# A list schedule with other durations for a hybrid decoder layer on one core

## The chip, the cores and the metric

The kernel runs on one core of one Trainium2 chip. The metric is the time of one execution on the device in microseconds (us). Engines are named as in the profile: PE (TensorE matmuls), PEld (its weight loads), DVE (VectorE), ACT (ScalarE), POOL (GpSimd), SP (SyncE, which here issues the DMAs).

## The reference

One decoder layer over 4096 tokens of width 1024. Three mixers read the same normalised and modulated input and share one input and one output projection:

```python
shift, scale, gate = jnp.split(c_act @ ada_w + ada_b, 3, axis=-1)
h = _rmsnorm(x, g_pre) * (1.0 + scale[:, None]) + shift[:, None]
proj = h @ w_in
aq, ak, av, ag, rkv, rg, gq, gkk, gv, gg = jnp.split(proj, ...)
attn = _sliding_window_attention(aq, ak, av, sinks) * jax.nn.silu(ag)   # window 128, 8 query heads, 2 key heads
rkv = rkv + (_shift(rkv) - rkv) * mu_rkv
rr, rk, rv = jnp.split(rkv, 3, axis=-1)
rwkv = _rwkv7_mixer(h, rr, rk, rv, ...) * jax.nn.silu(rg)               # 4 heads of 64, state 64x64 per head
gla = _gla_mixer(h, gq, gkk, gv, ...) * jax.nn.silu(gg)                 # 4 heads, chunks of 64
y = jnp.concatenate([attn, rwkv, gla], axis=-1) @ w_out
return x + gate[:, None] * _rmsnorm(y, g_post)
```

The RWKV mixer is a recurrence over tokens, `S = S * w + (S @ -kk) (kk*a) + v k`, with output `S @ r`; the kernel computes it in chunks of 64 tokens.

## The kernel before, in words

The 4096 tokens are cut into 16 tiles of 256. The program has two phases. Phase 1 (to about 1215 us) runs the two recurrent mixers for all tiles and, between their operations, turns the remaining weights into pairs of f16 slices for phase 2. Phase 2 computes attention, the gates and the output projection, one tile per period of about 65 us.

Names that are used below, in phase 1:

- `xt` is a tile of x (1 MB by DMA). `hf` are its squares (sums `ssx`) and later its scaled values, `msx`, `nwi`, `rsx`, `nwt` are the twelve small DVE operations of a reciprocal square root, `tp` its transposes on PE, `hT` the transposed normalised input as two f16 parts, stored in `hscr` for phase 2.
- `lp`, `zz`, `pv`, `gqk` are projections of hT on PE (weights as two f16 parts, so three matmuls for each slice). They share one ring of PSUM banks. `zb` is zz after the token shift (DVE); a bank is free for the next projection when zb is done.
- `gp`, `ga`, `gl`, `cgp` are the forget gate of GLA: gp (PE), ga (three ACT operations with a table load among them), gl (DVE), cgp its cumulative sum (PE).
- RWKV for each chunk: `atp` and `AT` (products within the chunk), `sp`, `Ss`, `Sst` (the state), `rp`, `rs`, `up`, and `UV` (ACT copies of up and vp, read by sp and `bp`). `T`, `TT`, `Xp`: the inverse of a triangular block. `tsc` and `TT` are its substitution on DVE, 30 small operations for a tile; it reads `AS`, which is AT's diagonal blocks sent through DRAM (`adr`) and back by DMA, with its diagonal set to one by POOL.
- `yt`, `ot`, `np`: transposes and norms of the outputs. `gap`, `kvp`, `op`, `Gst`: GLA's products and state.
- `cs`, `ch`, `cl`: a slice of weights by DMA, its high and low f16 part. The first ACT operation on cs, its square with a sum, is also named ch. `aw`, `acc`: the adaLN matrix (1 MB blocks, summed on POOL).
- `wps`, `gw`, `cw`: decay of RWKV.

In phase 2: `qp`, `kp`, `q`, `kT` (queries and keys), `sc`, `pr` (scores), `gp`, `gh`, `ag`, `mx`, `mT` (gates and mixed values), `op`, `yv` (output projection), `oi` (scale).

Every instruction goes through one helper (line 299 in the profile), so groups are told apart by tile names. The program is written by generators ("streams"), one for a stage of a tile; which generator goes on is set by a small model, and this order of writing is not what the engines run. `Order.note` records each instruction with a planned duration (`occ` is how long its engine is held, `lat` when its result is there), the instructions that it needs, and its tile's turn in a buffer. `Order.pin` then runs a list schedule over these records: it takes the engine that can begin first, picks the earliest recorded instruction that is ready, and ties each instruction to the one before it on its engine. So every engine's row is fixed by the table of durations; the instructions and their number are not. `pin` is called once for phase 1 and once for phase 2. The first stage of phase 2 is not pinned.

In the planner PE has tilings: 64x64 products occupy one quarter of the array, 128x128 products all of it, written (2, 2) and (4, 4) in units of 32. A change costs 0.094 us in the plan.

Of the kernel before, what the change touches and what calls it, by code (L numbers as in the profile page):

```python
# [31 lines left out]
HOP, VL, AL, PL = 0.4, 0.2, 0.2, 0.06  # L32
EXP_TABLE, LN_TABLE = 1, 2
LIFT = {}
LANES = ((0.06, 1.04e-3, VL), (0.02, 1.0e-3, AL), (0.1, 2.3e-3, 0.0), (0.0, 1e-3 / 2.4, PL), (0.05, 0.0, 2.0))

SIZE = {F16: 2, BF16: 2, F32: 4, I32: 4}
ENGINES = ("PE", "DVE", "Activation", "Pool", "SP")
HOP_FROM = {"PE": 0.037, "DVE": 0.034, "Activation": 0.034, "Pool": 0.06, "SP": 0.03}
HOP_INTO = {"PE": 0.02, "Pool": 0.04, "SP": 0.03}  # L40


# [12 lines left out]
class Step:  # L55


    __slots__ = ("ins", "eng", "occ", "lat", "table", "array", "bytes", "needs", "turn", "start", "end", "left", "then")


class Order:
# [1 line left out]


    def __init__(self, tc):
        self.tc, self.held, self.masks = tc, {}, {}
        self.steps = []
        self.wrote, self.read, self.users, self.slots, self.known = {}, {}, {}, {}, set()

# [25 lines left out]
    def note(self, eng, name, outs, ins, func, r):  # L95

        st = Step()
        st.ins, st.eng, st.table, st.array, st.bytes, st.then = r.ins, str(eng.engine).split(".")[-1], None, None, 0, []
        e, o = st.eng, outs[0]
        on_psum = [a for a in ins if str(a.tensor.space) == "PSUM"]  # L100
        n = max(math.prod(a.shape[1:]) for a in [o, *ins[:1]])
        cols = len([a for a in ins[1:] if math.prod(a.shape[1:]) == 1]) if n > 1 else 0
        if e == "PE":
            f32, lhs = ins[0].dtype == F32, self.region(ins[0])
            n = math.prod(o.shape[1:])
            _, p0, p1, _ = self.region(o)
            rows, cs = (lhs[1] // 32, (lhs[2] + 31) // 32), (p0 // 32, (p1 + 31) // 32)
            rows, cs = [(0, 4) if b - a > 2 else (a, b) for a, b in (rows, cs)]
            mode = (rows[1] - rows[0], cs[1] - cs[0])
            took = n * (2 if f32 else 1) / 2400 + 0.003  # L110
            took = max(took, 0.056 if not f32 else 0.109 if mode[1] == 4 else 0.0)
            issue = 0.007 if not f32 or mode == (4, 4) else 0.009 if mode == (1, 1) else 0.16 if mode == (2, 4) else 0.03
            cells = [4 * a + b for a in range(*rows) for b in range(*cs)]
            st.array = (mode, cells, 2 if f32 and name == "matmul" else 1, took, issue)
            st.occ = st.lat = 0.0
        elif e == "SP":
            st.bytes = math.prod(ins[0].shape) * SIZE[ins[0].dtype]
            kb = st.bytes / 1024
            st.occ = 0.47
            st.lat = next((t for k, t in ((8, 1.9), (64, 2.0), (128, 2.2), (256, 2.6), (512, 3.5)) if kb <= k), 4.8)  # L120
        elif e == "Activation":
            st.occ = (0.05 if on_psum else 0.093) + 0.093 * (len(ins) - 1) + 0.832e-3 * n
            st.lat = st.occ + 0.1
            if len(outs) > 1:
                st.occ += 0.187
                st.lat = st.occ + 0.02
            st.table = LN_TABLE if func == AF.Ln else EXP_TABLE if func in (AF.Exp, AF.Tanh) else None
        elif e == "Pool":
            if name == "memset":
                st.occ = 0.06  # L130
            elif name == "tensor_copy":
                st.occ = 0.25 if n <= 2 else 0.11 + 0.95e-3 * n
            else:
                st.occ = 0.42 + 1.35e-3 * n if n <= 256 else 1.95e-3 * n
            st.lat = st.occ + 0.05
        else:
            if name == "tensor_reduce":
                n = math.prod(ins[0].shape[1:])
            fast = name in ("tensor_scalar", "tensor_single_scalar") and not on_psum and o.dtype == F32
            fixed, rate = 0.065 + 0.06 * (cols > 0), 1.04e-3  # L140
            if fast:
                rate = 0.53e-3
            elif name == "transpose":
                fixed = 0.09
            elif name == "memset":
                fixed, rate = 0.05, 0.3e-3
            elif name == "tensor_tensor" and len(o.shape) == 3 and o.shape[2] <= 16 and n > 16:
                fixed, rate = 0.09, 1.55e-3
            st.occ = fixed + rate * n
            st.lat = st.occ + 0.085  # L150

        k, st.needs, st.turn = len(self.steps), {}, []
        out_r, in_r = [self.region(a) for a in outs], [self.region(a) for a in ins]
        tiles = {a.tensor.name: a.tensor for a in [*outs, *ins]}

        def need(j, data=False):
            st.needs[j] = st.needs.get(j, False) or data

        for t, tensor in tiles.items():
            if t not in self.known:  # L160
                self.known.add(t)
                if t in self.held and tensor.tag:
                    held = self.slots.setdefault((tensor.owner_uid, tensor.tag), [])

                    if held and self.users.get(held[-1]):
                        st.turn.append(self.users[held[-1]][0])
                    if len(held) == self.held[t]:
                        for j in self.users.get(held.pop(0), ()):
                            need(j)
                    held.append(t)  # L170
            elif t in self.held and self.users.get(t):
                st.turn.append(self.users[t][0])
            if str(tensor.space) == "PSUM":
                for j in self.users.get(t, ()):
                    need(j)

        def meet(a, b):
            return a[1] < b[2] and b[1] < a[2] and (a[3] is None or a[3] & b[3])

        def covered(a, b):  # L180
            return b[1] <= a[1] and a[2] <= b[2] and (a[3] is None or not a[3] & ~b[3])

        for a in in_r:
            for w, j in self.wrote.get(a[0], ()):
                if meet(a, w):
                    need(j, True)
        for a in out_r:
            if a[3] is not None:
                for old in (self.wrote, self.read):
                    for w, j in old.get(a[0], ()):  # L190
                        if meet(a, w):
                            need(j)
                    old[a[0]] = [(w, j) for w, j in old.get(a[0], ()) if not covered(w, a)]
            self.wrote.setdefault(a[0], []).append((a, k))
        for a in in_r:
            self.read.setdefault(a[0], []).append((a, k))
        for t in tiles:
            self.users.setdefault(t, []).append(k)
        st.needs.pop(k, None)
        self.steps.append(st)  # L200
# [7 lines left out]
    def pin(self):  # L208
# [7 lines left out]
            if not st.left:  # L216
                ready[st.eng][k] = 0.0
        free = dict.fromkeys(ENGINES, 0.0)
        cells, mode, table, pipe = [0.0] * 16, None, None, 0.0
        last = {}  # L220
        for _ in steps:
            e = min((e for e in ENGINES if ready[e]), key=lambda e: max(free[e], min(ready[e].values())))
            now = max(free[e], min(ready[e].values())) + 1e-9
            k = min(k for k, t in ready[e].items() if t <= now)
            st, t = steps[k], max(free[e], ready[e].pop(k))
            if e == "PE":
                m, at, passes, took, issue = st.array
# [5 lines left out]
                    cells[c] = t + passes * took  # L233
                free[e], st.end = t + issue * passes, t + passes * took + 0.165
            else:
                if st.table is not None and st.table != table:
                    t, table = max(t, free[e] + 1.28), st.table
                free[e], st.end = t + st.occ, t + st.lat
                if st.bytes > 100e3:
                    pipe = max(pipe, t + 1.7) + st.bytes / 310e3  # L240
                    st.end = max(st.end, pipe)
            st.start = t
# [21 lines left out]
class Model:  # L264


    def __init__(self, tc):
        self.tc, self.lift, self.order = tc, 0, Order(tc)
        self.wrote, self.read, self.banks = {}, {}, {}
        self.now = 0.0  # L270

# [14 lines left out]
class Lane:  # L286
# [6 lines left out]
    def __getattr__(self, name):  # L293
        f = getattr(self.eng, name)

        def call(*args, **kw):
# [4 lines left out]
            aps = [a for a in (*args, *kw.values()) if isinstance(a, bass.AP)]  # L301
            outs = [aps[0].tensor.name] + ([kw["accum_out"].tensor.name] if kw.get("accum_out") is not None else [])
            accum = kw.get("accum_out")
            self.model.order.note(self.eng, name, aps[:1] + ([] if accum is None else [accum]),
                                  [a for a in aps[1:] if a is not accum], next((a for a in args if isinstance(a, AF)), None), r)
            m, t = self.model, self.clock if self.serial else self.model.now
# [50 lines left out]
def hybrid_kernel(ctx, tc, x, vecs, rows, adaw, w1, wl, w2, wo, w2aug, a2, gk2, cst, ctr, ctg, abias, out):  # L357
# [149 lines left out]
    def emit():  # L507

        while live:
# [10 lines left out]
            assert best is not None, [(s[2], s[1], s[4]) for s in live]  # L520
            PE.clock = max(PE.clock, when)
            model.now = PE.clock
            model.lift = LIFT.get(best[2], 0)
            need = next(best[3], done)
            if need is done:
                done.add((best[2], best[1]))
# [1280 lines left out]
```

## Time and profile before

| | before |
|---|---|
| median of 3 runs | 2227.8 us (2226.26 to 2230.65) |
| profiled execution, its own time | 2226.16 us |
| its span, first to last instruction | 2224.4 us |
| mean granted TensorE clock | 0.983 |
| PE busy | 2063.7 us (93%) |
| DVE busy | 1513.7 us (68%) |
| ACT busy | 1111.6 us (50%) |
| POOL busy | 191.6 us (9%) |
| ACT table loads | 65, 1283 ns each |

A timeline row reads: start in us, duration, engine, line, operation, what it writes and reads, shapes, count, and in brackets how long the engine had been idle before it and what ended that. In a row of waits the numbers are the total in us, how often, and the longest.

### The profile page before, as it was taken

Reading aid. Unit: us, or ns where it says so; the run is one execution under the profiler, and the core shown is the slowest. Engines: PE = TensorE matmul, PEld = TensorE weight load, DVE = VectorE, ACT = ScalarE, POOL = GpSimd, SP = SyncE. Lnnn points to the kernel's source line nnn. Section 1 sums busy time; section 2 is a strip of 40 time slices with the busy share of each in tenths; the row PEclk is TensorE's granted clock in tenths of the full one; section 3 lists DMA queues with packets and bytes.
Section 4 is the critical chain, followed back from the end, with each engine's and each line's share of the span. In section 5 each row is a group of like instructions: output and inputs, shape, how many; then the busy total and the mean of one; then the engine's idle time right before and its main releaser. Section 6 shows DMA issues by size and latency. Waiting matters only on the chain. (4 is left out here: it accounts for less than half of the span.)

```text
span 2224.4 us, 61651 instructions
## 1 busy us (share of the span) xinstructions
PE 2063.7 (93%) x25417; PEld 1755.6 (79%) x25417; DVE 1513.7 (68%) x4970; ACT 1111.6 (50%) x2627; POOL 191.6 (9%) x364
## 2 busy tenths in 40 slices
PE   1599999999999999999997999999999999999996
PEld 1478877777777777787776888888888888888885
DVE  7767787777778777666665676666666666666764
ACT  3566666676766765555423434343434434343441
POOL 0241100111111111111000000000000000000000
PEclk9899999999999999999998999999999999999998
DMA  7332233323233322102324121222221121212111
GB/s 292 118 100 94 80 97 100 97 88 111 77 103 102 97 90 71 54 16 76 124 76 137 63 89 51 70 70 76 71 78 62 56 68 67 78 69 80 61 42 38
DMA packets 149092, 188.46 MB, mean 85 GB/s; under 512 B 49458, under 2 KB 120648, under 8 KB 142408
## 3 DMA queue, kind: packets, MB, share of 16 engines
q1 hardware_dynamic: 146776, 182.23, 24.9%
q8 instruction: 201, 3.29, 0.6%
q10 hardware_dynamic: 2032, 2.26, 0.3%
q14 instruction: 83, 0.68, 0.1%
HBM read 126.75 MB, written 57.68 MB: 83 GB/s over the span
## 5 line engine op out<-in xcount | busy, mean ns | idle before, releaser
L299 PEld LDWEIGHTS <-mT 128*128 128x128 f16 x3072 | 301.3, 98 | 40.1 <-ACT mT L299 2.6
L299 ACT ACTIVATE pr<-pr,nm,lsc 128x256 f32<-128x256 f32 (+1 forms) x256 | 149.3, 585 | 88.7 <-DVE nm L299 86.7
L299 ACT ACTIVATE ag<-gp,gh 128x512 f32<-128x512 f32 x64 | 43.6, 682 | 185.5 <-PE gp L299 185.4
L299 PEld LDWEIGHTS <-hT 128*128 128x128 f16 x1536 | 119.5, 100 | 18.9 <-DVE hT L299 1.0
L299 DVE CUSTOM_DVE_ANT_0 pr<-sc,ab,sinks 128x256 f32<-128x256 f32 (+1 forms) x256 | 107.8, 477 | 37.6 <-PE sc L299 35.9
L299 DVE SCALAR_TENSOR_TENSOR ag<-ag,gp 128x512 f32<-128x512 f32 x64 | 43.5, 679 | 110.7 <-ACT ag L299 110.6
L299 PE MATMUL pv<-gvh,hT 128*128 128x272 f16 x512 | 100.4, 287 | 0.7 <-DVE hT L299 0.4
L299 PE MATMUL lp<-hT,Lh 128*128 128x256 f16 x512 | 96.1, 279 | 2.4 <-ACT vg L299 2.4
L299 PE MATMUL op<-o0h,mT 128*128 128x256 f16 x512 | 93.4, 276 | 3.6 <-ACT mT L299 2.5
L299 PE MATMUL zz<-hT,kh 128*128 128x256 f16 x512 | 92.3, 276 | 0.0
L299 PE MATMUL gp<-hT,q3h 128*128 128x256 f16 x512 | 88.0, 278 | 3.6 <-PEq L1669 3.6
L299 PE MATMUL op<-o3h,mT 128*128 128x256 f16 x512 | 91.4, 273 | 0.0
L299 ACT ACTIVATE jy<-yv 128x1024 f16<-128x1024 f32 x32 | 33.8, 1057 | 114.0 <-DVE yv L299 114.0
L299 PE MATMUL gqk<-hT,gqkh 128*128 128x256 f16 x512 | 88.1, 273 | 1.9 <-DVE zb L299 1.9
L299 PE MATMUL qp<-hT,q1h 128*128 128x256 f16 x512 | 85.5, 274 | 4.2 <-DVE kT L299 4.2
L299 PE MATMUL op<-o2h,mT 128*128 128x256 f16 x512 | 89.3, 273 | 0.0
L299 PE MATMUL op<-o1h,mT 128*128 128x256 f16 x512 | 89.1, 273 | 0.0
L299 POOL COPY kT<-kT 128x512 f16<-128x512 f16 x15 | 10.1, 676 | 909.6 <-DVE kT L299 853.1
L299 PE MATMUL zz<-hT,rh 128*128 128x256 f16 x512 | 86.7, 273 | 0.0
L299 PE MATMUL zz<-hT,vh 128*128 128x256 f16 x512 | 86.4, 273 | 0.0
L299 ACT ACT_TABLE_LOAD x65 | 83.4, 1283 | 5.4 <-DMA sinks<-in_rows 4.2
L299 PE MATMUL gp<-hT,q4h 128*128 128x256 f16 x512 | 85.7, 273 | 0.0
(385 smaller groups left out, 6318.8 us busy)
## 6 DMA issues: line engine op xcount, KB each, us to landing
xt<-in_x SPq DMA_DIRECT2D x16, 1024.0 KB, 5.0
hscr<-hT SPq DMA_DIRECT2D x16, 1024.0 KB, 7.0
hT<-hscr SPq DMA_DIRECT2D x16, 1024.0 KB, 4.8
xo<-in_x SPq DMA_DIRECT2D x16, 1024.0 KB, 5.5
out<-yv SPq DMA_DIRECT2D x32, 512.0 KB, 3.0
cs<-in_w SPq DMA_DIRECT2D x112, 128.0 KB, 2.2
stg<-in_adaw SPq DMA_DIRECT2D x8, 1024.0 KB, 7.6
cs<-in_wo SPq DMA_DIRECT2D x64, 128.0 KB, 2.2
```

Source lines behind the costliest of these rows:

```text
L299: r = f(*args, **kw)
```

## The change

Only the planner's numbers and its rule of choice change; the instructions are the same. A result that lands by DMA is planned 0.6 us later than its landing, instead of 0.03. The landing times of small DMAs are finer. All DMAs, not only those over 100 KB, go through one queue of 310 KB/us in the plan. On ACT and DVE an instruction that works on another half of the partitions than the one before it is planned 0.115 us later. On PE, a ready instruction of the tiling in force is taken before an earlier one of another tiling, unless the array is in tiling (4, 4) and another has waited for 0.6 us. `LAG` is empty, so `rank` is the order of recording.

```diff
+LAG = {}
+TILING_WAIT = 0.6
-HOP_FROM = {"PE": 0.037, "DVE": 0.034, "Activation": 0.034, "Pool": 0.06, "SP": 0.03}
+HOP_FROM = {"PE": 0.037, "DVE": 0.034, "Activation": 0.034, "Pool": 0.06, "SP": 0.6}
...
+        st.half, st.rank = None, len(self.steps) + self.lag
...
-            st.lat = next((t for k, t in ((8, 1.9), (64, 2.0), (128, 2.2), (256, 2.6), (512, 3.5)) if kb <= k), 4.8)
+            st.lat = next((t for k, t in ((8, 1.9), (32, 2.0), (128, 2.3), (256, 2.6), (512, 3.5)) if kb <= k), 4.8)
...
+        if e in ("Activation", "DVE"):
+            st.half = (out_r[0][1], in_r[0][1] if e == "Activation" and in_r and out_r[0][2] - out_r[0][1] <= 64 else None)
...
-            k = min(k for k, t in ready[e].items() if t <= now)
+            at = sorted((k for k, t in ready[e].items() if t <= now), key=lambda k: (steps[k].rank, k))
+            k = at[0]
+            if e == "PE" and mode is not None and steps[k].array[0] != mode:
+                same = [q for q in at if steps[q].array[0] == mode]
+                wait = max(now - ready[e][q] for q in at if steps[q].array[0] != mode)
+                if same and (mode != (4, 4) or wait < TILING_WAIT):
+                    k = same[0]
...
+                if st.half is not None:
+                    was, half[e] = half.get(e, st.half), st.half
+                    if was[0] != st.half[0] or None not in (was[1], st.half[1]) and was[1] != st.half[1]:
+                        t = max(t, free[e] + 0.115)
...
-                if st.bytes > 100e3:
+                if st.bytes:
                     pipe = max(pipe, t + 1.7) + st.bytes / 310e3
```

In phase 1 about 13% of PE's rows, 19% of DVE's, 16% of ACT's and 12% of SP's stand elsewhere than before. In phase 2 the rows of PE, ACT, POOL and SP are the same, and DVE's differ in one row of each period and two more at the second tile. Three places (L299 and L317 are the same helper line in the two files):

ACT around the gate `ga` of a middle tile (the one that ran at 597 us), before:

```order
L299 ACTIVATE ch_8947,wss8_8665<-cs_8881 128x256
L299 ACTIVATE ch_9005,wss8_8665<-cs_8949 128x256
L299 ACTIVATE ch_9077,wss8_8665<-cs_9007 128x256
L299 ACTIVATE ga_8871<-gp_8914 128x256
L299 ACTIVATE ga_8871<-ga_8871 128x256
L299 ACT_TABLE_LOAD
```

and in the change:

```order
L317 ACTIVATE ch_8947,wss8_8665<-cs_8881 128x256
L317 ACTIVATE ga_8871<-gp_8914 128x256
L317 ACTIVATE ch_9005,wss8_8665<-cs_8949 128x256
L317 ACTIVATE ga_8871<-ga_8871 128x256
L317 ACTIVATE hf_8942<-tp_8937,sh_77,gs_76 128x256
L317 ACT_TABLE_LOAD
```

The first ga stands ahead of two squares that wait for DMAs of cs. At the same place on PE, before:

```order
L299 MATMUL up_8974<-rs_8934,tf0_503 64x64 x4
L299 LDWEIGHTS Lh_329
L299 MATMUL lp_8840<-hT_7822,Lh_329 128x256
L299 MATMUL cgp_8981<-CTG_139,gl_8869 128x129 x2
L299 MATMUL tp_8995<-ident_63,xt_8688 128x128 x4
```

and in the change, where twelve lp follow up_8974, of which the last is shown:

```order
L317 LDWEIGHTS Ll_330
L317 MATMUL lp_8840<-hT_7822,Ll_330 128x256
L317 MATMUL vp_9043<-ident_63,zb2_8420 128x128 x4
L317 MATMUL cgp_8981<-CTG_139,gl_8869 128x129 x2
L317 MATMUL tp_8995<-ident_63,xt_8688 128x128 x4
```

Eleven lp and a group of vp moved ahead of cgp.

DVE around the state `Sst` of the tile that ran at 420 us, before:

```order
L299 TENSOR_TENSOR Ss_5821<-sp_5816,Sst1_495 128x128
L299 TENSOR_TENSOR tsc_5737<-TT_5735,AS_5731 128x8x2
L299 TENSOR_TENSOR Sst0_494<-Ss_5821,cd_3960 128x128
L299 TENSOR_REDUCE TT_5735<-tsc_5737 128x8
L299 TENSOR_TENSOR tsc_5737<-TT_5735,AS_5731 128x8x3
```

and in the change:

```order
L317 TENSOR_TENSOR Ss_5821<-sp_5816,Sst1_495 128x128
L317 TENSOR_REDUCE wss_5843<-wss8_5337 128x1
L317 TENSOR_TENSOR Sst0_494<-Ss_5821,cd_3960 128x128
L317 TENSOR_TENSOR qb_5306<-gap_5848,gmask_132 128x256
L317 TENSOR_TENSOR qb_5306<-gap_5849,gmask_132 128x256
L317 TENSOR_TENSOR tsc_5737<-TT_5735,AS_5731 128x8x2
L317 COPY rs_5867<-rp_5854 128x128
```

Sst and two qb stand ahead of the first tsc, and rs right behind it instead of fourteen rows later. The tile at 354 us has the same exchange of Sst and tsc.

DVE in the second tile's start (about 120 to 133 us), before:

```order
L299 TENSOR_TENSOR nwt_1309<-rsx_1307 128x2
L299 SCALAR_TENSOR_TENSOR nwt_1309<-nwt_1309,msx_1305 128x2
L299 SCALAR_TENSOR_TENSOR zb0_912<-zz_913,mu_c_467,zs_993 128x256 x2
L299 TENSOR_TENSOR cd_1046<-ep_967,em_968 128x2x3
L299 COPY cd_1046<-ep_967 128x2
L299 COPY em0_1047<-em_968 128x2
L299 SCALAR_TENSOR_TENSOR rsx_1307<-nwt_1309,rsx_1307 128x2
```

and in the change:

```order
L317 SCALAR_TENSOR_TENSOR nwt_1309<-nwt_1309,msx_1305 128x2
L317 SCALAR_TENSOR_TENSOR rsx_1307<-nwt_1309,rsx_1307 128x2
L317 TENSOR_SCALAR xt_1195<-xt_1195,rsx_1307 128x1024
L317 SCALAR_TENSOR_TENSOR zb0_912<-zz_913,mu_c_467,zs_993 128x256 x2
L317 TENSOR_TENSOR cd_1046<-ep_967,em_968 128x2x3
```

zb0 moved behind the rest of the chain and the first half of xt's scaling. On SP at that time, before:

```order
L299 DMA aw_525<-in_adaw 128x2048
L299 DMA aw_537<-in_adaw 128x2048
L299 DMA xt_1195<-in_x 128x2x1024
L299 DMA gscr_72<-gr_521 1x256
L299 DMA aw_549<-in_adaw 128x2048
L299 DMA hscr_71<-hT_732 128x4096
```

and in the change:

```order
L317 DMA aw_525<-in_adaw 128x2048
L317 DMA xt_1195<-in_x 128x2x1024
L317 DMA aw_537<-in_adaw 128x2048
L317 DMA gscr_72<-gr_521 1x256
L317 DMA hscr_71<-hT_732 128x4096
L317 DMA aw_549<-in_adaw 128x2048
```

Two aw blocks went behind the load of xt and the store of hT.

More of the change, by code (lines that the diff above doesn't have):

```diff
@@ L55 @@
 class Step:
-    __slots__ = ("ins", "eng", "occ", "lat", "table", "array", "bytes", "needs", "turn", "start", "end", "left", "then")
+    __slots__ = ("ins", "eng", "occ", "lat", "table", "array", "bytes", "half", "rank", "needs", "turn", "start", "end", "left", "then")
 class Order:
     def __init__(self, tc):
-        self.tc, self.held, self.masks = tc, {}, {}
+        self.tc, self.held, self.masks, self.lag = tc, {}, {}, 0
         self.steps = []
@@ L218, in pin @@
         free = dict.fromkeys(ENGINES, 0.0)
-        cells, mode, table, pipe = [0.0] * 16, None, None, 0.0
+        cells, mode, table, pipe, half = [0.0] * 16, None, None, 0.0, {}
         last = {}
@@ L267, in __init__ @@
     def __init__(self, tc):
-        self.tc, self.lift, self.order = tc, 0, Order(tc)
+        self.tc, self.lift, self.stage, self.order = tc, 0, None, Order(tc)
         self.wrote, self.read, self.banks = {}, {}, {}
@@ L303, in call @@
             accum = kw.get("accum_out")
+            self.model.order.lag = LAG.get(self.model.stage, 0)
             self.model.order.note(self.eng, name, aps[:1] + ([] if accum is None else [accum]),
@@ L522, in emit @@
             model.now = PE.clock
-            model.lift = LIFT.get(best[2], 0)
+            model.lift, model.stage = LIFT.get(best[2], 0), best[2]
             need = next(best[3], done)
```

## The prediction

> **What bounds the kernel now.** I read the page's busy times and slices first, then windows along the span, then the engines' waits, then short timelines.
>
> ```profile
> PE 2063.7 (93%) x25417; PEld 1755.6 (79%) x25417; DVE 1513.7 (68%) x4970; ACT 1111.6 (50%) x2627; POOL 191.6 (9%) x364
> ```
>
> ```profile
> 60.00:120.00 60.00, 39.86 (x248) 30.37 (x247) 40.87 (x73) 34.88 (x58) 22.52 (x13) 0.83 0.38 140
> 540.00:600.00 60.00, 58.04 (x812) 47.79 (x809) 45.93 (x169) 39.54 (x93) 7.39 (x18) 1.00 0.33 101
> 660.00:720.00 60.00, 56.18 (x731) 46.07 (x723) 46.25 (x171) 41.01 (x92) 7.83 (x16) 1.00 0.32 99
> 1320.00:1380.00 60.00, 59.75 (x705) 53.37 (x704) 38.01 (x109) 25.44 (x65) 0.61 (x1) 1.00 0.18 58
> ```
>
> PE is the bound: 2063.7 us busy, 93% of the span. A window's row reads: stretch, length, then busy time and count of PE, PEld, DVE, ACT and POOL, granted clock, DMA share, GB/s. In phase 2 (1320:1380) PE has 0.25 us of 60 to give. In the middle of phase 1 it has 2 to 4 us of 60, and at 60:120 20 us. Only PE's order, and what PE waits for, can move the time; the instruction lists are the same, so PE's work is the same except for tiling switches and clock. What PE waited for between 120 and 1190 us (total, times, longest):
>
> ```profile
> PE cgp L299 <- DVE gl L299: 7.3, 6, 2.7
> PE rp L299 <- DVE Sst L299: 5.3, 3, 2.8
> PE yt L299 <- DVE ysb L299: 5.1, 4, 3.7
> PE Xp L299 <- DVE T L299: 4.6, 6, 0.9
> PE atp L299 <- DVE RA L299: 4.1, 4, 1.5
> PE ot L299 <- DVE osb L299: 3.3, 5, 1.0
> PE bp L299 <- ACT UV L299: 3.2, 7, 0.5
> PE sp L299 <- ACT UV L299: 2.3, 8, 0.3
> ```
>
> **Part 1: cgp and the recurrence in the middle tiles.** One such tile, at 597 to 601 us, PE, DVE and ACT:
>
> ```profile
> 597.81 0.38 PE L299 MATMUL lp<-hT,Lh 128*128 128x256 f16 x2
> 598.23 1.10 PE L299 MATMUL atp<-RA,KB 64*64 64x128 f32 x32
> 600.87 0.71 PE L299 MATMUL cgp<-CTG,gl 128*128 128x129 f32 x4 [1.10 <-DVE gl L299]
> 601.42 0.60 PE L299 MATMUL tp<-ident,xt 128*128 128x128 f32 x4
> 601.86 0.27 PE L299 MATMUL lp<-hT,Lh 128*128 128x256 f16 x1
> 601.97 0.27 PE L299 MATMUL lp<-hT,Ll 128*128 128x256 f16 x1
> ...
> 600.39 0.42 DVE L299 SCALAR_TENSOR_TENSOR gl<-gp,ga 128x256 f32<-128x256 f32 x1 [2.65 <-ACT ga L299]
> 600.74 1.28 DVE L299 TENSOR_TENSOR AT<-atp,rmask 128x512 f32<-128x512 f32 x2
> ...
> 596.73 0.42 ACT L299 ACTIVATE ch<-cs 128x256 f16<-128x256 f32 x1 [1.57 <-DMA cs<-in_wo]
> 598.65 1.28 ACT L299 ACT_TABLE_LOAD   x1
> ```
>
> The chain is: a weight slice cs lands, ACT squares it (ch, in order), then ga, a table load, ga, then DVE gl, then PE cgp. ACT sat 1.57 us at ch with ga queued behind it. Now ga stands one to two squares earlier, and on PE twelve lp and a group of four vp stand ahead of cgp instead of one lp. Successive lp start 601.97 - 601.86 = 0.11 us apart, so eleven more are 1.2; four transposes took 601.86 - 601.42 = 0.44. So PE has 1.6 us more to do, against waits of 0.3 to 2.7: most vanish. bp and sp (3.2 + 2.3), behind ACT's UV copies, likewise get lp and zz groups ahead of them. These three rows hold 12.8 us; I take **-10.0** (bounds 0, if ga waits elsewhere as long, and -12.8). Xp is placed as before and keeps its 4.6. What is late next is gl itself: the second AT (the pair took 1.28 us) now stands ahead of gl on DVE. Before, DVE sat idle for 2.65 us there, which covers it; without that cover gl is up to 0.65 late.
>
> **Part 2: the state Sst at two tiles.** DVE's tsc reads AS, which comes by DMA behind a whole xt load:
>
> ```profile
> 420.13 0.18 DVE L299 TENSOR_TENSOR tsc<-TT,AS 128x16 f32<-128x16 f32 x1 [4.20 <-POOL AS L299]
> 420.23 0.28 DVE L299 TENSOR_TENSOR Sst<-Ss,cd 128x128 f32<-128x128 f32 x1
> ...
> 419.98 0.12 POOL L299 MEMSET AS<- 128x16 f32 x1 [7.85 <-DMA AS<-adr]
> ...
> 420.57 0.37 PE L299 MATMUL rp<-Sst,RA 64*64 64x64 f32 x1 [2.80 <-DVE Sst L299]
> 424.70 0.69 PE L299 MATMUL up<-rs,tf 64*64 64x64 f32 x8
> ```
>
> Sst needed nothing but its turn, and stood behind tsc. Now it stands ahead, at this tile and at that of 354 us (PE waited 2.23 there), so both waits go. rs then stands behind the first tsc, so up can start shortly after 420.13 + 0.28 + 0.2, some 0.9 us after PE has done what stands before it; I give back 1.4 for both. After each wait the granted clock is at half:
>
> ```profile
> 355.00:356.00 1.00, 1.00 (x6) 0.28 (x3) 0.86 (x5) 0.77 (x2) 0.00 (x0) 0.50 0.21 74
> ...
> 422.00:423.00 1.00, 1.00 (x3) 0.61 (x3) 0.98 (x4) 0.00 (x0) 0.00 (x0) 0.50 0.01 4
> 425.00:426.00 1.00, 1.00 (x12) 0.76 (x9) 1.00 (x5) 0.52 (x2) 0.00 (x0) 0.50 0.00 0
> ```
>
> It is down from about 354.5 to 358 and from 420.5 to 426; half the rate over 3.5 and 5.5 us loses 4.5. So -5.0 - 4.5 + 1.4, taken as **-8.0** (bounds -3, if short waits remain and the clock falls all the same, and -9.5). The Trainium skill (TensorE: Matmul & The Clock Gate, part 1 on the clock gate) says that TensorE falls to half rate after an idle window of about 3.4 us and comes back after a busy one. By that rule waits of 2.2 and 2.8 us need not drop the clock, nothing of the 4.5 would belong to these waits, and the sum would be 4.5 us higher; the rows show half clock right behind them, so the trace decides for counting it, and the 3.5 us of the first stretch agree with the rule's length.
>
> **Part 3: the other waits of phase 1.** yt, atp and ot hold 12.5 us. In the new order one atp and one ot find filler ahead of them, the others stand as before: half, 6, and 2 from the small rows that I don't show. **-8.0** (bounds 0 and -14).
>
> **Part 4: tilings.** PE changes tiling 661 times instead of 671. Three lp up to the change to atp took 598.23 - 597.81 = 0.42 us, where three steps of 0.11 are 0.33, so a change is about 0.09: **-0.9**. The changes of half on DVE and ACT stay within five of what they were, and table loads stay at 65: nothing.
>
> **Part 5: the start.** Up to 97 us the order is the same. Then:
>
> ```profile
> 80.08 3.57 DVE L299 TENSOR_SCALAR msx<-ssx 128x2 f32<-128x2 f32 x1
> 83.68 0.17 DVE L299 TENSOR_SCALAR nwi<-msx 128x2 int32<-128x2 int32 x1
> ...
> 79.21 4.41 POOL L299 TENSOR_TENSOR aw<-aw,scol 128x2048 f32<-128x2048 f32 x1 [65.62 <-DMA aw<-in_adaw]
> ...
> 96.92 0.48 PE L299 MATMUL tp<-ident,xt 128*128 128x128 f32 x1 [13.79 <-DVE xt L299]
> ...
> 120.61 1.03 DVE L299 TENSOR_SCALAR msx<-ssx 128x2 f32<-128x2 f32 x1 [2.54 <-ACT hf L299]
> 128.30 0.87 DVE L299 SCALAR_TENSOR_TENSOR zb<-zz,mu_c,zs 128x256 f32<-128x256 f32 x2
> 131.56 1.42 DVE L299 TENSOR_SCALAR xt<-xt,rsx 128x1024 f32<-128x1024 f32 x2
> ```
>
> Operations on two elements a row take 0.17 us alone and up to 3.57 beside POOL's aw products, and end when a product ends (83.65 and 83.62). In the second burst of products (114 to 130 us) five of the chain's twelve ran before zb, which freed the bank that PE's gqk waited for (1.9 us). Now all twelve and one half of the xt scaling (0.71) stand ahead of zb, and two of the aw loads are issued later, so the burst starts later too. If the burst spares the chain, zb comes at 128.30 + 7 x 0.2 + 0.71, or 2.1 us late; if it stretches the rest of the chain as it did the first, up to 9. PE's other work covers some: **+4.0** (bounds +1 and +13, the latter with the half clock that the first pause left).
>
> **Part 6: phase 2.** PE's, ACT's and POOL's order is the same. On DVE one q subtract stands one small operation earlier in each period, and once a kT subtract stands behind the second yv:
>
> ```profile
> 1283.37 1.23 DVE L299 TENSOR_TENSOR yv<-yv,xo 128x1024 f32<-128x1024 f32 x1
> ...
> 1283.40 0.39 PE L299 MATMUL qp<-hT,q1h 128*128 128x256 f16 x2 [0.30 <-DVE kT L299]
> ```
>
> PE waits for that kT already, so **+1.2**, once (bounds 0 and +2.5).
>
> **Part 7: waits that the new order makes.** Not in this trace. Up to 0.65 a tile by the AT of part 1 in six tiles, of which I take a third, 1.3, and one pair of AT (1.28) elsewhere: **+3.0** rounded up (bounds +1 and +9).
>
> Sum: -10.0 - 8.0 - 8.0 - 0.9 + 4.0 + 1.2 + 3.0 = **-18.7**. The profiled execution took 2226.16 us, so 2207.5; the median of the runs, 2227.8, stands 1.6 above it, so **2209** in the runs' terms. About 0.2%, 4.5 us, can be told from no change here.
>
> **Rivals.**
> (a) The waits move and are not saved. In a list schedule each engine's row is one long compromise: where cgp finds its filler, the lp used for it are missing later. For it: PE had work for every wait that went, so the later stretches are thinner by that work; Xp and most of the tail are unchanged. Against it: over 540:1080 PE has slack only in those short waits. Then parts 1 and 3 fall to a quarter, -4.5 instead of -18, and the time is 2222.5; with the start at its dear end it is no change.
> (b) The start collides in full: +13 instead of +4. For it: the first burst did just that, 13.79 us. Against it: before, half of the second burst was over when the chain began. The time is 2218. [...]
> (c) More goes: every wait of parts 1 to 3 to its bound, start +1, 2226.2 - 12.8 - 9.5 - 14 - 0.9 + 1 + 1.2 + 1, or 2192, 2194 in the runs' terms.
> (d) Slower: ACT's grouping by half and its longer view of landings make the UV copies of the recurrence stand behind a pair of hf or a table load (1.28 us), tile after tile. UV feeds sp, then Ss, Sst, rp, rs, up, and back: a delay of 1.28 plus one hf (about 0.55) is 1.8 a tile, times 16 tiles 29 us, so 2238. It decides from 18.7 / 16 = 1.2 us a tile. Against it: ACT's count of half changes hardly moves, and the UV copies stand among the same neighbours in the rows that I compared.
>
> **How the numbers follow.** The forecast, with parts 1 to 3 mostly as summed, 0.66; (a) 0.13; (b) 0.07; (c) 0.06; (d) 0.08. Faster by over 0.2%: the forecast, (b), (c) and a small part of (a), 0.80. Within 0.2%: most of (a), 0.11. Slower: (d) and a rest for what I don't see, 0.09. The range leaves out (d) and the far ends: 2194, which is (c), to 2226, where (a) ends.
>
> **What would show it.** Right: waits of cgp, bp and sp under 4 us together between 120 and 1190; no wait of rp for Sst near 352 and 418, and clock 1.00 in the windows behind them; phase 2's period unchanged with PE at 59.7 of 60; the gqk wait at 130 us longer than 1.9. Wrong: the same slack per 60 us at 540 to 900 under other names; a new wait of over 5 us at 115 to 140 with half clock after; UV copies late in every tile.

## The result, and the profile after

The changed kernel takes 2203.0 us (median of 4 runs, 2198.2 to 2208.7) against 2227.4 (4 runs): a ratio of 0.9889, 95% interval 0.9863 to 0.9915. The profiled execution took 2203.83 us. In two of the three later sessions, each on a chip of its own, the same pair gave 0.9880 (0.9853 to 0.9906) and 0.9885 (0.9867 to 0.9903). The forecast was 2209, with a range of 2194 to 2226.

The page's busy line after:

```profile
PE 2058.5 (93%) x25417; PEld 1757.3 (80%) x25417; DVE 1504.4 (68%) x4970; ACT 1109.4 (50%) x2627; POOL 198.3 (9%) x364
```

and the windows for the same stretches:

```profile
60.00:120.00 60.00, 41.00 (x273) 31.43 (x274) 43.99 (x78) 37.46 (x65) 20.10 (x12) 0.80 0.37 140
540.00:600.00 60.00, 58.94 (x815) 48.95 (x813) 45.94 (x168) 40.77 (x98) 9.96 (x20) 1.00 0.31 92
660.00:720.00 60.00, 58.93 (x814) 48.74 (x809) 46.58 (x168) 41.40 (x98) 9.82 (x20) 1.00 0.32 99
1320.00:1380.00 60.00, 59.74 (x706) 53.40 (x704) 40.75 (x123) 25.92 (x66) 0.61 (x1) 1.00 0.21 72
```

The counts of instructions are the same. In the middle of phase 1 PE idles 1.1 us of 60, where it was 2.0 and 3.8; phase 2 is as it was. PE's waits between 120 and 1190 us after:

```profile
PE gp L317 <- issue: 5.0, 1, 5.0
PE ovp L317 <- DVE pr L317: 4.9, 3, 2.8
PE Xp L317 <- DVE T L317: 4.4, 5, 0.9
PE up L317 <- DVE rs L317: 3.4, 4, 1.2
PE yt L317 <- DVE ysb L317: 3.1, 3, 1.8
PE atp L317 <- DVE RA L317: 2.7, 4, 1.2
PE ot L317 <- DVE osb L317: 2.6, 4, 1.0
PE kp L317 <- ACT ysb L317: 2.1, 3, 1.0
...
PE rp L317 <- DVE Sst L317: 1.1, 3, 0.7
PE cgp L317 <- DVE gl L317: 1.0, 1, 1.0
```

cgp fell from 7.3 to 1.0, rp<-Sst from 5.3 to 1.1, and bp and sp (5.5 together) are gone from the list. up<-rs and kp<-ysb have grown. The row of ovp is the start of phase 2, which now falls into this window; before, ovp waited 5.2 us for pr, after 1190. A wait of gp for "issue" (time in which the engine waited for nothing that the profile shows), 5.0 us at one place, is new. The kind of wait is not: the list of before has

```profile
PE Xq L299 <- issue: 3.0, 2, 2.6
```

of which the 2.60 us stand at 1096.7, in the tail of phase 1.

Where the time went is read by comparing the start of the same instruction in the two timelines (the last cgp of a tile in phase 1, mp in phase 2):

| | before, us | after, us | difference |
|---|---|---|---|
| first cgp | 107.9 | 105.9 | -2.0 |
| third cgp | 210.7 | 207.5 | -3.2 |
| sixth | 403.9 | 392.7 | -11.2 |
| eleventh | 731.2 | 711.6 | -19.6 |
| last cgp | 1050.1 | 1021.0 | -29.1 |
| first mp of phase 2 | 1235.2 | 1212.6 | -22.6 |
| last mp | 2186.8 | 2164.4 | -22.4 |

Some 2 us a tile are won over all of phase 1, 29 by its last gate. From there to the first mp 6.5 are given back: 5.7 in the tail of phase 1 (to the first ovp, 1192.9 before and 1169.5 after) and 0.8 in the first stage of phase 2. The rest of phase 2 changes nothing.

A middle tile after (ACT, DVE, PE):

```profile
582.10 0.38 ACT L317 ACTIVATE ga<-gp 128x256 f32<-128x256 f32 x1 [2.16 <-PE gp L317]
582.38 0.41 ACT L317 ACTIVATE ch<-cs 128x256 f16<-128x256 f32 x1
583.65 1.28 ACT L317 ACT_TABLE_LOAD   x1
...
584.06 1.29 DVE L317 TENSOR_TENSOR AT<-atp,rmask 128x512 f32<-128x512 f32 x2 [1.56 <-PE atp L317]
585.40 0.42 DVE L317 SCALAR_TENSOR_TENSOR gl<-gp,ga 128x256 f32<-128x256 f32 x1
...
585.48 0.60 PE L317 MATMUL vp<-ident,zb 128*128 128x128 f32 x4
585.91 0.67 PE L317 MATMUL cgp<-CTG,gl 128*128 128x129 f32 x4
```

ga now waits for its own input and no longer for a weight slice; DVE works at AT in the time in which it sat idle; and vp fills PE up to cgp, which waits for nothing.

The state after, at the two tiles with the late AS: the first tsc still waits for it (1.48 and 1.05 us), but Sst has long gone:

```profile
341.65 0.29 DVE L317 TENSOR_TENSOR Sst<-Ss,cd 128x128 f32<-128x128 f32 x1
345.71 0.18 DVE L317 TENSOR_TENSOR tsc<-TT,AS 128x16 f32<-128x16 f32 x1 [1.48 <-POOL AS L317]
345.80 0.28 DVE L317 COPY rs<-rp 128x128 f32<-128x128 f32 x1
409.67 0.18 DVE L317 TENSOR_TENSOR tsc<-TT,AS 128x16 f32<-128x16 f32 x1 [1.05 <-POOL AS L317]
```

and the clock stays whole in the windows behind them:

```profile
350.00:355.00 5.00, 5.00 (x61) 4.33 (x61) 4.79 (x20) 1.79 (x6) 0.10 (x1) 1.00 0.00 0
415.00:420.00 5.00, 5.00 (x65) 4.19 (x64) 4.79 (x27) 2.19 (x6) 0.19 (x1) 1.00 0.01 3
```

The start after (DVE, POOL, PE):

```profile
116.13 0.17 DVE L317 TENSOR_SCALAR msx<-ssx 128x2 f32<-128x2 f32 x1 [1.79 <-ACT hf L317]
116.93 3.45 DVE L317 SCALAR_TENSOR_TENSOR nwt<-nwt,msx 128x2 f32<-128x2 f32 x1
124.50 0.87 DVE L317 SCALAR_TENSOR_TENSOR zb<-zz,mu_c,zs 128x256 f32<-128x256 f32 x2
...
116.75 3.62 POOL L317 TENSOR_TENSOR aw<-aw,scol 128x2048 f32<-128x2048 f32 x1 [3.68 <-DMA aw<-in_adaw]
...
125.42 0.38 PE L317 MATMUL gqk<-hT,gqkh 128*128 128x256 f16 x2 [0.79 <-DVE zb L317]
```

POOL had to wait 3.68 us for its aw block, which is loaded later, and its burst starts at 116.75 instead of 114.15. The first four small operations of the chain run at 0.17 us, two of the twelve are stretched (3.45 and 2.20), and zb comes at 124.5 instead of 128.3. The chain itself starts earlier, at 116.13 instead of 120.61. Part of that is the order of ACT, where the second square of xt stood behind ep before, which waited for PE, and now follows the first square:

```profile
118.88 0.39 ACT L299 ACTIVATE ep<-cw 128x260 f32<-128x260 f32 x1 [1.63 <-PE cw L299]
119.43 1.06 ACT L299 ACTIVATE hf<-xt 128x1024 f16<-128x1024 f32 x1
...
114.95 1.06 ACT L317 ACTIVATE hf<-xt 128x1024 f16<-128x1024 f32 x1
```

And the place in the tail that gives time back, PE and the DMA queues in two windows before it ended:

```profile
1122.27 0.86 PE L317 MATMUL Xq<-td,Xs 32*32 32x32 f32 x64
1128.18 0.58 PE L317 MATMUL gp<-hT,q4h 128*128 128x256 f16 x2 [5.05 <-issue]
```

```profile
q1 hardware_dynamic: 264, 0.96, 89.1%
...
q1 hardware_dynamic: 364, 0.45, 61.3%
q8 instruction: 1, 0.02, 3.0%
```

The first of these rows is 1121 to 1125, the other two are 1125 to 1127. PE waited for no semaphore. From 1119 on, three loads of 512 KB (q5l, q6h, q6l) keep the DMA engines busy (89% from 1121 to 1125, without a packet of instructions); then one packet of the instruction queue passes, in the window that ends 1.2 us before PE goes on. The granted clock is 0.50 from 1128 to 1134, so the place costs 5 us and about 3 more. The 2.60 us of the kernel before look the same: two loads of 512 KB (q3h, q3l) and a store are in flight up to 1094, then one packet of the instruction queue passes (1094.3 to 1095.2), and PE goes on at 1096.74.

### The profile page after: what moved, and what is told of

Its sections match the earlier page's. It is cut to its first block, busy times and chain, and to the rows that moved or that the text cites. A ratio compares the mean times of both kernels' runs of the same rounds, so it can differ in the third digit from the quotient of the medians.

```text
span 2202.1 us, 61608 instructions
## 1 busy us (share of the span) xinstructions
PE 2058.5 (93%) x25417; PEld 1757.3 (80%) x25417; DVE 1504.4 (68%) x4970; ACT 1109.4 (50%) x2627; POOL 198.3 (9%) x364
## 5 line engine op out<-in xcount | busy, mean ns | idle before, releaser
L317 PEld LDWEIGHTS <-mT 128*128 128x128 f16 x3072 | 301.4, 98 | 39.2 <-ACT mT L317 2.6
L317 ACT ACTIVATE pr<-pr,nm,lsc 128x256 f32<-128x256 f32 (+1 forms) x256 | 149.3, 585 | 87.8 <-DVE nm L317 87.1
L317 ACT ACTIVATE ag<-gp,gh 128x512 f32<-128x512 f32 x64 | 43.7, 682 | 188.2 <-PE gp L317 188.2
L317 PEld LDWEIGHTS <-hT 128*128 128x128 f16 x1536 | 118.2, 99 | 19.0 <-DVE hT L317 1.5
L317 DVE CUSTOM_DVE_ANT_0 pr<-sc,ab,sinks 128x256 f32<-128x256 f32 (+1 forms) x256 | 107.8, 477 | 37.3 <-PE sc L317 35.6
L317 DVE SCALAR_TENSOR_TENSOR ag<-ag,gp 128x512 f32<-128x512 f32 x64 | 43.4, 678 | 111.3 <-ACT ag L317 111.3
L317 PE MATMUL pv<-gvh,hT 128*128 128x272 f16 x512 | 98.6, 284 | 1.8 <-DVE kg L317 0.8
L317 PE MATMUL lp<-hT,Lh 128*128 128x256 f16 x512 | 94.9, 279 | 3.0 <-ACT vg L317 3.0
L317 PE MATMUL op<-o0h,mT 128*128 128x256 f16 x512 | 93.5, 276 | 2.8 <-ACT mT L317 2.5
L317 PE MATMUL gp<-hT,q3h 128*128 128x256 f16 x512 | 89.0, 280 | 7.5 <-issue 4.0
L317 PE MATMUL zz<-hT,kh 128*128 128x256 f16 x512 | 93.6, 274 | 0.0
L317 PE MATMUL gp<-hT,q4h 128*128 128x256 f16 x512 | 87.5, 277 | 5.0 <-issue 5.0
L317 POOL COPY kT<-kT 128x512 f16<-128x512 f16 x15 | 9.2, 612 | 920.3 <-DVE kT L317 869.8
L317 PE MATMUL op<-o3h,mT 128*128 128x256 f16 x512 | 91.4, 273 | 0.0
L317 ACT ACTIVATE jy<-yv 128x1024 f16<-128x1024 f32 x32 | 33.8, 1057 | 113.8 <-DVE yv L317 113.8
L317 PE MATMUL qp<-hT,q1h 128*128 128x256 f16 x512 | 85.8, 275 | 5.4 <-DVE kT L317 5.4
L317 PE MATMUL op<-o2h,mT 128*128 128x256 f16 x512 | 89.3, 273 | 0.0
L317 PE MATMUL op<-o1h,mT 128*128 128x256 f16 x512 | 89.1, 273 | 0.0
L317 PE MATMUL gqk<-hT,gqkh 128*128 128x256 f16 x512 | 87.8, 273 | 0.8 <-DVE zb L317 0.8
L317 PE MATMUL zz<-hT,rh 128*128 128x256 f16 x512 | 86.8, 273 | 0.0
L317 PE MATMUL zz<-hT,vh 128*128 128x256 f16 x512 | 86.7, 273 | 0.0
```

The costliest lines, as they stand in the source:

```text
L317: r = f(*args, **kw)
```

## The experiments

Theory S held that slack for landings carries the gain, theory T the tiling rule, theory M that no single edit does; Q, F and E are about single places. The ratios are to the kernel before, which ran beside them: the first four in one session, the next four and the last four in two others, each session on a chip of its own.

**Slack alone.**

```diff
-HOP_FROM = {..., "SP": 0.03}
+HOP_FROM = {..., "SP": 0.6}
```

> The kernel before with one number changed: a result that lands by DMA is planned 0.6 us later than its landing, not 0.03. Theory S (most of the gain is that work waiting for DMAs - ACT's squares of weight slices, DVE's tsc - no longer stands ahead of the gates and the state on the in-order engines): 12 to 18 us faster than before, cgp's 7.3 us of waits under 3, rp<-Sst's 5.3 under 2. Theory T (the gain comes from filler that the tiling rule keeps together on PE): within 4 us of before, cgp's waits stay at 6 to 8. Theory M (no single edit carries it; any corrected number moves a few waits): 4 to 8 us faster.

0.9946 (0.9928 to 0.9964), 12 us faster by the medians. cgp's waits are gone from the list; but the wait behind tsc only moved, at 354 us to rs and at 422 to qb, which now stood behind tsc:

```profile
354.71 0.69 PE L299 MATMUL up<-rs,tf 64*64 64x64 f32 x8 [4.21 <-DVE rs L299]
...
422.87 1.22 PE L299 MATMUL kvp<-vg,kt 128*128 128x256 f32 x2 [3.51 <-DVE qb L299]
```

Theory S was right on cgp and wrong on the state.

**Changes of half alone.** The other three edits set back.

```diff
+                        t = max(t, free[e] + 0.115)
```

> The kernel before with the 0.115 us for a change of partition half alone. Theory S and theory T: within 3 us of before. Theory M: 4 to 8 us faster.

1.0023 (1.0008 to 1.0038): slower by 0.23%, 3.4 us by the medians. cgp keeps 6.7 us, and up<-rs and kvp<-qb wait 4.2 and 3.6. No theory had this sign.

**Tiling rule alone.**

```diff
+                if same and (mode != (4, 4) or wait < TILING_WAIT):
+                    k = same[0]
```

> The kernel before with the rule alone that PE keeps its tiling while another has waited under 0.6 us. Theory S: within 4 us of before (fewer changes of tiling, 0.09 us each, about ten of them). Theory T: 12 to 18 us faster, with lp and zz groups ahead of cgp. Theory M: 4 to 8 us faster.

0.9959 (0.9945 to 0.9973), 9 us faster, between the theories. cgp is gone from its list too; tp<-hf grew from 1.3 to 5.8 us (210 to 1047 us), and up<-rs waits 4.0 at 357.

**Queue and landing times alone.**

```diff
-                if st.bytes > 100e3:
+                if st.bytes:
-  ((8, 1.9), (64, 2.0), (128, 2.2), ...
+  ((8, 1.9), (32, 2.0), (128, 2.3), ...
```

> The kernel before with all DMAs in one planned queue and the finer landing times, nothing else. Theory S: part of the same effect, 4 to 8 us faster, with Sst ahead of the first tsc at 354 and 420 us. Theory T: within 4 us of before. Theory M: 4 to 8 us faster.

0.9937 (0.9920 to 0.9955), 15 us faster, more than any theory gave it. Here the long stall behind tsc is gone (tsc waits 1.45 and 1.94 us, and PE only 1.15 us for rs, at 415), and cgp's waits are not:

```profile
PE cgp L317 <- DVE gl L317: 7.1, 5, 2.5
```

So two mechanisms are apart: cgp's waits go by slack or by the tiling rule, the long stall at AS by the queue.

**Without the queue.** The changed kernel with the rule and the table of before.

```diff
-                if st.bytes:
+                if st.bytes > 100e3:
```

> The changed kernel with the one-queue rule and the landing table of before, the other three edits kept. Theory Q (the stall behind tsc at the tiles of 354 and 420 us goes only if the plan knows that AS lands behind a whole xt; slack of 0.6 us moves it to rs and qb): waits of up for rs near 4 us at 350 and of kvp for qb near 3.5 us at 415, half clock after them, 8 to 12 us slower than the changed kernel. Rival (0.6 us of slack is enough with the tiling rule beside it): within 3 us of the changed kernel.

0.9917 (0.9892 to 0.9943) beside 0.9880 for the changed kernel: 6.7 us slower by the medians, less than Q said, and the intervals overlap; at 414 us PE waits only 1.08 us. The trace is plainer than the times: the long wait is back at 350 us, though at Sst and not at rs.

```profile
349.91 0.36 PE L317 MATMUL rp<-Sst,RA 64*64 64x64 f32 x1 [4.09 <-DVE Sst L317]
...
350.00:352.00 2.00, 2.00 (x22) 1.17 (x23) 1.73 (x9) 1.19 (x3) 0.00 (x0) 0.50 0.05 20
```

Half clock stands behind it, as in the kernel before.

**The changed kernel again.** No edit.

> The changed kernel itself, for comparison with the three beside it on one chip: 0.987 to 0.991 of before. If the 5.05 us in which PE waits for no semaphore at 1128 us is a late instruction fetch, it is there again, within 1 us; if it was an accident of one execution, it is gone.

The wait at gp was there again, 3.91 us, and in a third trace 4.14. It belongs to the program. Something else came back too, at the first of the two tiles with the late AS: from the issue of its load until POOL could set its diagonal AS took 7.3 us (343.77 to 351.05) where it took 5.5 in the first trace, tsc waited 3.37 us for it, and rs behind it held up PE, with half clock after that. Why the load took longer is not shown.

```profile
351.64 0.45 PE L317 MATMUL up<-rs,tf 64*64 64x64 f32 x8 [2.89 <-DVE rs L317]
...
353.00:355.00 2.00, 2.00 (x9) 1.42 (x6) 1.61 (x8) 1.06 (x4) 0.00 (x0) 0.50 0.05 12
```

So the change makes this stall shorter in two of its three traces and does not remove it. In the traces of kernels with the queue rule PE's longest wait near 350 us is 0.4 to 2.9 us (none with the queue alone), in the five without it 2.2 to 4.2.

**Without changes of half.**

```diff
-                        t = max(t, free[e] + 0.115)
+                        t = max(t, free[e] + 0.0)
```

> The changed kernel without the 0.115 us for a change of half. Alone that edit took 0.23% more time than before. Theory M (the edits add up): 3 to 7 us faster than the changed kernel. Rival (in company it pays): 2 to 6 us slower.

0.9891 (0.9864 to 0.9918) beside 0.9880, medians 2207.69 and 2207.66: no difference in the time of the whole kernel. Alone the edit costs; what it does in company is read by stage, at the end of this section.

**Without the last weight load.**

```diff
-        order = (2, 0, 1, 3, 4, 5, 6)
+        order = (2, 0, 1, 3, 4, 5)
...
+        got[6] = (got[4][0], got[4][1], w_inv[6])
```

> The changed kernel without the load of the last pair of gate weights (q6h and q6l, 1 MB; its products use q4's tiles, so the last quarter of the gates is computed from other weights). Theory F (at 1122 to 1128 us PE waits for an instruction fetch that comes through DMA engines filled by q5l, q6h and q6l): the wait of gp at 1128 falls from 5 to under 1 us, the half clock behind it goes too, 5 to 8 us faster than the changed kernel. Rival (PE waits there for something else, or the fetch is late by its own timing): the wait stays within 1 us and the time within 2.

The load that is left out holds the last quarter's gate weights, so this kernel's gates are wrong there; only its time is of use. 0.9866 (0.9838 to 0.9895), 4.7 us less than the changed kernel by the medians, not settled by the intervals. The wait is shorter, not gone:

```profile
1130.49 0.58 PE L317 MATMUL gp<-hT,q4h 128*128 128x256 f16 x2 [2.09 <-issue]
```

In all four traces of these two programs PE goes on 1.2 to 1.5 us after an instruction packet has passed, and in the kernel before 1.55 us, at 1096.7. That points to a wait for instructions, which is argued from this timing and not tested by itself. The last pair of loads makes 2 to 3 of its 4 to 5 us; the rest has a cause that these runs don't show.

**Without slack, and without the tiling rule.**

```diff
-HOP_FROM = {..., "SP": 0.6}
+HOP_FROM = {..., "SP": 0.03}
```

> The changed kernel with landings planned 0.03 us late again, the other three edits kept. cgp's waits went in both kernels that had slack alone or the tiling rule alone. Theory E (either of the two is enough for cgp, so their gains don't add): cgp stays under 2 us in all, and the kernel is within 5 us of the changed one. Rival (slack carries most): cgp's waits are back at 4 us or more and it is 8 to 14 us slower than the changed kernel.

```diff
-                if same and (mode != (4, 4) or wait < TILING_WAIT):
+                if False:
```

> The changed kernel without the rule that PE keeps its tiling. Theory E: cgp stays under 2 us, within 5 us of the changed kernel, some ten more changes of tiling. Rival (the rule carries most): cgp's waits at 4 us or more, 8 to 12 us slower than the changed kernel.

0.9911 (0.9898 to 0.9924) and 0.9908 (0.9893 to 0.9922), beside 0.9885 (0.9867 to 0.9903) for the changed kernel: 8 and 6 us slower by the medians, though the intervals touch. cgp stays off both lists, so theory E is right that either edit is enough for it; but each is worth a little more than 5 us by the medians, in other places. Without slack tp waits for ACT (205 to 1050 us):

```profile
PE tp L317 <- ACT hf L317: 6.6, 5, 2.9
PE up L317 <- DVE rs L317: 5.4, 7, 2.8
```

The third trace of the changed kernel stood beside these:

> The changed kernel again, for comparison with the three beside it on one chip: 0.986 to 0.990 of before; a wait of up for rs of 1 to 3 us near 350, since AS still lands behind a whole xt there.

up waits for rs 0.41 us at 348 and 0.64 at 413, less than expected.

**xt behind AS.** The planner is told that an xt load doesn't start ahead of the last recorded AS load.

```diff
+        kind = o.tensor.name.split("_")[0]
+        if e == "SP" and kind == "AS":
+            self.landed = k
+        if e == "SP" and kind == "xt" and self.landed is not None:
+            st.turn.append(self.landed)
```

> The changed kernel, with a tile's xt load issued behind the last AS load that was recorded ahead of it. Before, at three tiles xt went first and AS landed behind its 1 MB. Theory Q: AS lands some 3 us earlier at 350, 415 and late in phase 1, tsc holds nothing up, up's wait for rs goes below 1 us in all, 2 to 6 us faster than the changed kernel. Rival (xt comes later now and ACT, which squares it in order, waits longer): waits of tp, gp or sp for ACT take the place, within 2 us of the changed kernel or slower.

0.9880 (0.9864 to 0.9897), median 2205.7 beside 2205.8: no difference. up<-rs fell from 4.0 to 2.3 us in all, but two waits of sp for UV took the place, as the rival said; ACT had hf, which waits for xt, ahead of UV:

```profile
353.14 0.45 PE L322 MATMUL sp<-UV,BK 128*64 128x64 f32 x8 [1.80 <-ACT UV L322]
416.92 0.45 PE L322 MATMUL sp<-UV,BK 128*64 128x64 f32 x8 [1.11 <-ACT UV L322]
```

In the tail the wait for issue moved from gp to Xq (4.67 us). No version tried is clear of the changed kernel on the fast side.

**By stage.** The time of the whole kernel mixes what an edit does in the middle of phase 1 with the wait for issue in its tail, which comes and goes with the order. The same starts of instructions as above, one trace for each figure, in us:

| | third to last cgp | last cgp to first mp | wait of gp for issue |
|---|---|---|---|
| before | 839.4 | 185.1 | none |
| changed, three traces | 813.5, 817.3, 814.9 | 191.6, 190.8, 189.9 | 5.05, 3.91, 4.14 |
| without the queue | 824.2 | 186.8 | none |
| without changes of half | 827.2 | 184.2 | none |
| without slack | 830.4 | 184.9 | none |
| without the tiling rule | 822.1 | 189.2 | 2.65 |
| slack alone | 835.9 | 183.1 | none |
| half alone | 845.3 | 189.0 | 2.97 |
| tiling rule alone | 836.6 | 185.4 | none |
| queue alone | 833.9 | 186.5 | none |

In the middle every edit pays in company: without it the stretch is 5 to 17 us longer, against 4 us between the three traces of one program. Alone they win 3.5, -5.9, 2.8 and 5.5 us there, 6 together, where all four in company win 22 to 26. The half rule costs alone and pays in company; the medians hid it, because the kernel without it doesn't have the wait at gp. Its profiled execution stood 4.6 us above its median, so its figure of 10 to 14 us may be that much too high.

## Why the prediction was right, and where its terms were wrong

The sum said -18.7 and the profiled executions differ by 2226.16 - 2203.83 = 22.3. Sign, size and the place of most of it hold; single terms don't, and that the sum came so near is in part luck. The start was forecast 4.0 us dearer and came out 3.2 cheaper, most of which is the clock of that execution; the tail gave back 6.5 that no term had. The two misses cancelled.

- **Part 1 (-10.0):** cgp lost 6.3 us and bp and sp 5.5, so -11.8, near the bound of -12.8. ACT's squares no longer hold up ga, and the filler covers the rest. The 0.65 of AT ahead of gl did not show: in the tile above, AT ended at 585.35, and gl followed at once.
- **Part 2 (-8.0):** in the first trace the wait fell by 4.2 us and up<-rs rose by 2.4, where 1.4 was given back; the 4.5 us of half clock went. That is -6.3. In the second trace of the changed kernel less was won, since up waited 2.89 us at the first tile and half clock followed. The clock column at 350 and 415 us is 1.00 in the first trace, and 0.50 again in that second one and in the kernel without the queue rule, each time behind a long wait, so half clock belonged to the wait. By the Trainium skill's rule (TensorE: Matmul & The Clock Gate, part 1 on the clock gate) only idle windows of about 3.4 us drop it; the trace of before had the drop behind 2.2 and 2.8 us, and the measurement decides. The length of the window agrees with the steps of 3.41 us in the last section, but the window ahead of a drop need not be idle: PE was busy for 1.19 of 3.42 us in the one at 351 to 355 us.
- **Part 3 (-8.0):** yt, atp and ot fell from 12.5 to 8.4. With the small rows the sum is right for the middle: the listed waits of PE went from 35.3 us (210 to 1050) to 17.2 (207 to 1021), 18.1 in all, 4.5 of clock beside them, of 25.9 won there. Of the last 3 us some 1 is in waits too short for the list: PE's whole idle time fell by 19.0. The other 2 are in PE's busy time, which fell by 6.9, of which the clock is 4.5; changes of tiling may be among them.
- **Part 4 (-0.9)** can't be told apart at this size.
- **Part 5 (+4.0) failed.** The step was zb reckoned from its old 128.30, as if the chain began when it had begun before, and "the burst starts later too" taken as harm. zb came 3.8 us earlier, not 2 to 9 later, and gqk waited 0.79 us for it, not over 1.9. About 2 of the 3.8 are the clock's. The rest is the chain's start: in the second and third trace, where the clock was as before, it began at 118.3 and 118.5 instead of 120.61, because the second square of xt no longer stands behind ep on ACT, and zb came at 126.6 and 126.7. The burst stretched two of the twelve operations in all three traces (3.4 and 2.2 us). Two more traces of the changed kernel have the first cgp at 108.4 and 108.5 and the third at 210.9 and 210.2, so the 2.0 and 3.2 won there in its first trace are mostly the clock after the pause at 83 to 97 us (0.96 from 100 to 104 us in that execution, 0.50 in the two others and before), and the order's own part is about nothing. Rival (b) did not come.
- **Part 6 (+1.2):** the wait of qp for kT grew from 0.30 to 1.37 us, as costed, and the next mp was only some 0.1 us later: a smaller wait behind it gave it back.
- **Part 7 (+3.0):** up<-rs and kp<-ysb grew by 3.5 together. But the 2.4 of up<-rs are in part 2 already, so about 1.1 is left beside small new rows such as pv's 0.8, and the term was too large. What it did not have is the wait for issue in the tail. With its half clock it comes to some 8 us, more than the 6.5 that were given back, since other waits of the tail got shorter (yt 4.4 to 3.1, Xq 2.6 to 1.2). No row of before pointed to this place, but the row of Xq showed that such waits occur, and the prediction left it out.

Rivals (a) and (d) are excluded by the middle windows and the list, and (c) was not reached: yt, atp and ot kept 8.4 of their 12.5. (a) describes the single edits well, though: three of the four moved the stall behind tsc to rs or qb, and the half rule alone made the kernel slower.

## What to carry to other kernels

Where a planner fixes each engine's order, look in the trace for the instruction that stands in front of a queue and waits for a DMA: what it costs is the work behind it, on its own engine and on those that this work feeds. A landing must be planned with the transfers ahead of it in the same queue; a constant slack moves such a wait to the next row, as slack alone did here. Corrections of a list schedule neither add up nor keep their sign one by one, so measure them together and alone, compare stage by stage and not only the whole time, and look at the windows of the clock behind each wait, since a wait of 3 us can cost 5.

## What the runs showed of the hardware

In these traces the granted clock changes only in steps of 3.41 us: the times of its changes within one trace lie whole multiples of that apart. Whether it drops goes with how busy PE was in one such window, and not with the length of a wait alone. In the fourteen traces here, PE was busy for less than 0.41 of the time in 87 windows at whole clock, and each was followed by one at half clock; between 0.41 and 0.6 it was 27 of 82, and above 0.6 one of some 8270. Why one between 0.41 and 0.6 drops and another does not stays open. In the kernel before, the wait of 2.23 us at 354 fell into one window, and the wait of cgp of 2.71 us at 666 was split over two, behind which the clock stayed at 1.00 (the figure behind the length is PE's busy time):

```profile
351.26:354.68 3.42, 1.19 (x28) 0.77 (x28) 0.85 (x6) 1.58 (x4) 0.12 (x1) 1.00 1.00 386
354.68:358.09 3.41, 3.41 (x21) 1.86 (x22) 3.14 (x14) 1.42 (x5) 0.00 (x0) 0.50 0.14 52
...
661.88:665.29 3.41, 1.94 (x46) 1.46 (x43) 0.00 (x0) 2.58 (x7) 0.00 (x0) 1.00 0.27 78
665.29:668.70 3.41, 2.13 (x26) 1.77 (x26) 2.43 (x5) 3.33 (x10) 1.49 (x2) 1.00 0.07 7
```

A program that waits for no semaphore can still stand for 4 to 5 us, while transfers of 1.5 MB and then a packet of its instruction queue pass; that the wait is for these instructions is argued, not shown. And the same program reached its first gate at 105.9, 108.4 and 108.5 us in three executions, with the time at which the clock comes back after a pause of 11.5 to 13.8 us.
